# Down projection of a hybrid decoder block: four of 22 chunk pairs in Strassen's form, segment sums kept in DRAM

## The chip, the cores and the metric

The kernel runs on one core of one Trainium2 chip. A core has five engines, each with its own instruction queue: TensorE (PE, matrix multiply, with PEld for its weight loads), VectorE (DVE), ScalarE (ACT), GpSimd (POOL) and SyncE (SP, which here only issues DMAs). Matmuls read SBUF and write PSUM, which has eight banks of 128 x 512 fp32. DVE and ACT read both memories. The metric is the device time of one launch in microseconds (us); before the change it is 1165.92 us, the median of three runs (1165.78 to 1165.96).

## The reference, cut to what matters

One decoder block on x of 256 tokens and 2048 features, in fp32, with one conditioning vector c:

```python
mod = silu(c) @ w_ada + b_ada                     # 2048 x 12288
sh1, sc1, g1, sh2, sc2, g2 = split(mod, 6)
h = rms_norm(x, norm1_g) * (1 + sc1) + sh1
q, k, v, gb, gc, xt = split(h @ w_in, ...)        # 2048 x 6144
attn = causal attention of 8 heads of 128
conv = gb * causal_dwconv(gc * xt, conv_w, conv_b)
x = x + g1 * (concat(norm(attn), norm(conv)) @ w_out)      # 2048 x 2048
h2 = rms_norm(x, norm2_g) * (1 + sc2) + sh2
u_gate, u_up = split(causal_dwconv(h2 @ w_ffn_up, ...), 2) # 2048 x 11264
x = x + g2 * ((silu(u_gate) * u_up) @ w_ffn_down)          # 5632 x 2048
```

The change is in the last product, the down projection: a 256 x 5632 matrix G (the gated activations) times w_ffn_down, 5632 x 2048.

## The kernel before

All of the kernel is one unrolled program. Its matrix work is cut into numbered **slots**, 202 of them before the change. A slot takes one tile of weights (up to four blocks of 128 x 512, 1 MB), loaded from DRAM by SP into one of the `raw` buffers. Every fp32 operand is split into a high and a low part in the format fp32r, and a product is three passes: low part of one operand times high part of the other and the reverse, and high times high. `split_hi` (line 255) makes the high part of a weight tile on ACT, `split_lo` (line 264) the low part on DVE and then asks for the next load (`load_next`). The splits of slot i + 2 are written in the program ahead of the matmuls of slot i (or behind them, for slots in the list `x_first`; the list `hi_late` puts `split_hi` behind the slot's small tasks). `hi` and `lo` have three buffers each, `raw` has six, and a pool of 38 tiles of 128 x 512 fp32 (`t2k`) holds nearly everything else. `CFG` (line 32) is a list of orders and offsets; `at(i, f)` puts a small task into slot i, and its class in `cls` says whether it comes ahead of the splits, and in which order. The main loop (line 1323) writes all of this out slot by slot, so the order on each engine's queue is fixed.

Slots 0 to 47 are the input projection, 48 to 63 the output projection. Then comes the FFN. Its 5632 inner columns are 44 chunks of 128, in 22 **groups** of two chunks. The groups are done in four **segments** (`segs`: 8, 5, 5 and 4 groups). In each segment first comes the up projection of its groups, four slots of about 16 matmuls of 512 columns and 16 of 256 each per group; after it `up_sum`, `up_conv`, `up_silu` and `up_gate` (line 774) finish the group on ACT and DVE and leave its two chunks of G, transposed and split into high and low, in `gT`. Then comes the down projection of the segment: for each column block f of 512 (four of them, taken in the pairs 0 and 1, 2 and 3) slots of up to four chunks, with two row blocks of 128 tokens. A column block has one PSUM bank for each row block, and accumulates over the segment's chunks in `mm_tok` (line 413): for each chunk and row block two passes with the high part of the weights, and after all of them one with the low part. At the end of a segment `evac_down` (line 789) copies a bank into an SBUF tile `dacc` (segment 0, ACT) or adds it (segments 1 and 2, DVE). Ahead of the last segment's sums `gate_down` (line 812) multiplies `dacc` by the gate g2 and adds x; in the last segment `evac_down` multiplies the bank by g2, adds that, and stores. For the last column block g2 is multiplied into the weights instead (`fold`).

The loads of the adaLN weights (`w_ada`, 96 tiles of 1 MB) are spread over the slots by the list `ada`, and DVE or PE accumulates them (`Ada.consume`, line 310). The gate vector g2 is accumulated on DVE in one `raw` buffer during the FFN and spread to all partitions by two small rounds of DMAs on POOL (`sum_rows`, `spread`). PSUM banks come from one pool of eight (`bank`, line 146): four for a group of the up projection, two for each column block of the down projection. A tile that is asked for takes a free buffer of its pool and waits, if need be, for the buffer's last user.

Of the kernel before, what the change touches and what calls it, by code (L numbers as in the profile page):

```python
# [31 lines left out]
CFG = {'ada': [[0, 2, 256, False, 0, 5], [4, 8, 512, False, 64, 8], [5, 0, 2048, False, 109, 18], [3, 8, 512, False, 55, 9],  # L32
# [3 lines left out]
 'bufs': [38, 6, 6, 3, 5],  # L36
# [12 lines left out]
 'segs': [8, 5, 5, 4],  # L49
# [3 lines left out]
 'qk': [[2, 5], [3, 7]],  # L53
# [4 lines left out]
 'slag': [[1, 3], [22, 25]],  # L58
 'hold': [1, 1, 0],
 'evac': [2, 1, 1],  # L60
 'sq': [5, 8, 2],
 'tr': [3, 7, 3],
 'part': 2,
 'up': [[0, 0, 1], [1, 3, 3], [0, 0, 1], [0, 3, 3]],
 'gate': [-16, -17, -6, -9],
# [15 lines left out]
         'evac_down': -1,  # L81
# [23 lines left out]
         'sum_rows': 1},  # L105
 'up0': [[0, 2, 4], [0, 3, 3], [0, 2, 2], [0, 1, 2], [2, 2, 4], [2, 4, 6], [0, 1, 2], [0, 0, 5], [3, 4, 4],
         [0, 2, 3]],
# [15 lines left out]
 'first_hi': True,  # L123
# [1257 lines left out]
```

## Time and profile before

| | us |
|---|---|
| median of 3 runs | 1165.92 |
| the profiled execution, its own time | 1165.9 |
| its span in the trace | 1164.1 |
| PE busy | 1148.0 |
| DVE busy | 920.7 |
| ACT busy | 617.1 |
| POOL busy | 16.9 |
| DMA moved | 320.11 MB, 275 GB/s in the mean |

The span is the time from the first to the last instruction in the trace; some 1.8 us of the device time lie around it. "Busy" is the sum of an engine's instruction times without overlaps. The groups of instructions of the costliest lines are the splits (line 267 on DVE, 445.8 us for 201 of them; line 261 on ACT, 373.9 us) and, on PE, the matmuls of the up projection (lines 861 and 864) and of `mm_tok` (lines 427, 429 and 430).

### The profile page before, as it was taken

The page shows a single profiled execution, that of the slowest core. Times are in us where ns is not written, and L with a number is a line of the kernel's source. Part 1 is how long each engine was busy: PE and PEld are TensorE (multiplying, and loading weights), DVE is VectorE, ACT ScalarE, POOL GpSimd, SP SyncE. Part 2 cuts the span into 40 slices and gives each one's busy share as a digit, 9 for nine tenths or more (in the row PEclk, how much of TensorE's full clock was granted, in tenths as well). Part 3 has the DMA queues.
Part 4 walks back from the last instruction along what each step waited for, and adds up shares of the span by engine and source line. Part 5 has one row for each costly group of instructions (what it writes and reads, how often), then busy time and mean ns, then how long its engine had stood idle before and what let it go on. Part 6 is the DMA issues. An engine that isn't in the chain of part 4 may idle for free.

```text
span 1164.1 us, 15680 instructions
## 1 busy us (share of the span) xinstructions
PE 1148.0 (99%) x6119; PEld 971.6 (83%) x6119; DVE 920.7 (79%) x1030; ACT 617.1 (53%) x889; POOL 16.9 (1%) x34
## 2 busy tenths in 40 slices
PE   6999999999999999999999999999999999999998
PEld 4677778888888889988888888888888888888887
DVE  4789989999999989889876468997556576577767
ACT  5644455667795465566664434545435454335451
POOL 1000000000000000000000000000000000000000
PEclk9999999999999999999999999999999999999999
DMA  9999989999899799975556479995675645675451
GB/s 364 407 416 394 412 328 357 404 351 347 304 357 335 268 333 353 351 252 174 185 191 217 172 273 340 329 344 184 213 233 182 217 163 202 227 235 186 148 178 73
DMA packets 188570, 320.11 MB, mean 275 GB/s; under 512 B 7360, under 2 KB 106132, under 8 KB 183888
## 3 DMA queue, kind: packets, MB, share of 16 engines
q1 hardware_dynamic: 186208, 314.60, 75.7%
q0 software_dynamic: 992, 2.35, 0.6%
q10 hardware_dynamic: 1296, 2.16, 0.5%
q8 instruction: 48, 0.79, 0.3%
q14 instruction: 26, 0.21, 0.0%
HBM read 314.87 MB, written 4.21 MB: 274 GB/s over the span
## 4 chain that ended last, share of the span: by engine, by line
PE 91%; DVE 4%; DMA 3%; ACT 1%; issue 0%; SPq 0%; DVEq 0%; ACTq 0%
PE z L861 25%; PE z L864 13%; PE z L847 4%; DMA raw<-in_w_in_dram 2%; DVE lo L267 2%; PE mk L429 1%; PE mk L430 1%; PE mk L427 1%; PE mx L429 1%; PE mc L429 1%; PE mq L430 1%; PE mg L429 1%; PE mq L429 1%; PE mc L430 1%; PE mx L430 1%; PE mv L429 1%
## 5 line engine op out<-in xcount | busy, mean ns | idle before, releaser
L267 DVE TENSOR_TENSOR lo<-raw,hi 128x2048 fp32r<-128x2048 f32 (+2 forms) x201 | 445.8, 2225 | 142.1 <-ACT hi L261 129.7
L261 ACT ACTIVATE hi<-raw 128x2048 fp32r<-128x2048 f32 (+2 forms) x201 | 373.9, 1865 | 306.7 <-PE z L861 62.9
L861 PE MATMUL z<-h,hi 128*128 128x512 f32 x1280 | 298.5, 390 | 0.0
L861 PEld LDWEIGHTS z<-h,hi 128*128 128x128 f32 x1280 | 237.8, 188 | 47.5
L325 DVE SCALAR_TENSOR_TENSOR ada<-raw,csil,ada 128x512 f32<-128x512 f32 (+3 forms) x167 | 195.9, 1176 | 4.7 <-DMA raw<-in_w_ada_dram 1.2
L864 PEld LDWEIGHTS z<-h,lo 128*128 128x128 f32 x1280 | 159.0, 192 | 4.0 <-issue 0.8
L864 PE MATMUL z<-h,lo 128*128 128x256 f32 x1280 | 160.3, 283 | 0.0
L725 DVE SCALAR_TENSOR_TENSOR uy<-ub,fc,uy 128x254 f32<-128x254 f32 (+1 forms) x176 | 71.4, 480 | 0.2
L757 DVE TENSOR_TENSOR ub<-z,ub 128x256 f32<-128x256 f32 x96 | 34.0, 417 | 36.6 <-ACT ub L754 36.6
L778 ACT ACTIVATE gh<-uy 128x512 fp32r<-128x512 f32 x22 | 13.9, 632 | 66.5 <-DVE uy L776 66.5
L847 PE MATMUL z<-h,hi 128*128 128x256 f32 x256 | 46.6, 285 | 0.4 <-ACT h L679 0.2
L720 ACT ACTIVATE uy<-ub,fc,fc 128x256 f32<-128x256 f32 x88 | 45.6, 601 | 0.0
L754 ACT ACTIVATE ub<-z 128x256 f32<-128x256 f32 x96 | 28.7, 384 | 27.0 <-PE z L861 26.9
L847 PEld LDWEIGHTS z<-h,hi 128*128 128x128 f32 x256 | 40.0, 192 | 0.8 <-ACT h L679 0.5
L847 PE MATMUL z<-h,lo 128*128 128x256 f32 x128 | 36.3, 284 | 0.0
L779 DVE TENSOR_TENSOR gl<-uy,gh 128x512 fp32r<-128x512 f32 x22 | 15.2, 693 | 15.4 <-ACT gh L778 15.4
L429 PE MATMUL mx<-hi,h 128*128 128x512 f32 x64 | 25.8, 403 | 0.4 <-ACT pa_g L439 0.4
L429 PE MATMUL mg<-hi,h 128*128 128x512 f32 x64 | 25.7, 402 | 0.0
L429 PE MATMUL mq<-hi,h 128*128 128x512 f32 x64 | 25.6, 399 | 0.0
L429 PE MATMUL mk<-hi,h 128*128 128x512 f32 x64 | 25.3, 395 | 0.0
L429 PE MATMUL mv<-hi,h 128*128 128x512 f32 x64 | 25.1, 392 | 0.0
L847 PEld LDWEIGHTS z<-h,lo 128*128 128x128 f32 x128 | 24.6, 192 | 0.0
(611 smaller groups left out, 1863.5 us busy)
## 6 DMA issues: line engine op xcount, KB each, us to landing
raw<-in_w_ada_dram SPq DMA_DIRECT2D x96, 1024.0 KB, 7.3
raw<-in_w_ffn_up_dram SPq DMA_DIRECT2D x176, 512.0 KB, 4.8
raw<-in_w_in_dram SPq DMA_DIRECT2D x47, 1024.0 KB, 8.0
raw<-in_w_ffn_down_dram SPq DMA_DIRECT2D x28, 1024.0 KB, 5.0
raw<-in_w_out_dram SPq DMA_DIRECT2D x16, 1024.0 KB, 6.6
raw<-in_w_ffn_down_dram SPq DMA_DIRECT2D x20, 768.0 KB, 4.3
xr<-in_x_dram SPq DMA_DIRECT2D x2, 1024.0 KB, 6.2
x<-in_x_dram SPq DMA_DIRECT2D x8, 256.0 KB, 7.5
```

The lines of the kernel that those rows point to most:

```text
L261: act(hi[:, :nk], t[:, :nk], AF.Copy)
L267: V.tensor_tensor(out=lo[:, :nk], in0=t[:, :nk], in1=hi[:, :nk].bitcast(F32), op=ALU.subtract)
L325: V.scalar_tensor_tensor(out=self.acc, in0=t[:, j, :], scalar=csil[:, i:i + 1], in1=self.acc, op0=ALU.mult, op1=ALU.add)
L429: mm(o, a, hi[:, k, s], start=(first and k == 0), stop=False)
L430: mm(o, b, hi[:, k, s], start=False, stop=False)
L720: act(y[:, s], b[:, s], AF.Identity, bias=bias[:, i + j:i + j + 1], scale=w[2][:, i + j:i + j + 1])
L725: V.scalar_tensor_tensor(out=o[:, d:], in0=v[:, :256 - d], scalar=w[2 - d][:, i + j:i + j + 1], in1=o[:, d:], op0=ALU.mult, op1=ALU.add)
L754: act(c[ft // 2][:, (ft % 2) * 256:(ft % 2) * 256 + 256], zp[grp][ft][:, 256:], AF.Copy)
L757: V.tensor_tensor(out=d, in0=zp[grp][ft][:, :256], in1=d, op=ALU.add)
L847: mm(o, w[:, j, a], h2T[k + j][:, v * 256:v * 256 + 256], start=begins and j == 0 and w is hi and not v, stop=ends and j == 3 and w is lo)
L861: mm(zp[grp][ft], hi[:, j, ft * P:(ft + 1) * P], h2T[k + j], start=begins and j == 0, stop=ends and j == 3)
L864: mm(zp[grp][ft][:, :256], lo[:, j, ft * P:(ft + 1) * P], h2T[k + j][:, :256], start=False, stop=False)
```

## The change

The groups 0, 9, 12 and 14 become **units**. For a unit and one half of the columns (1024 of 2048, `cp`) the product of two row blocks, two chunks and two column blocks is computed as in Strassen's algorithm (in Winograd's variant) with seven block products in place of eight. The sums of blocks of G are made in `up_gate` (tiles `gs`, split again into high and low, seven stationary blocks in `gS`). The sums of weight blocks are made in `split_lo` on DVE, in place in the raw tile: such a tile is used twice, in a slot "A" with three of its blocks as loaded (three products), and in a slot "B" with four sums (four products). A slot B has no load of its own.

The seven products go into seven sums, j of 0 to 6; the ordinary groups ("s") of a segment add their four block products to the sums 0, 1, 3 and 7. So a column half of segments 0 to 2 now uses eight banks. The order of the groups within a segment is written out in `orders`; the two column halves follow each other. Where a sum is complete, `evac_sum` copies its bank to SBUF (ACT for the j in `unit_act`, otherwise DVE), and a DMA on POOL writes it to DRAM, or adds it to what is there (`accum_op`). Near the end of segment 2 and the start of segment 3's up projection `join_load` loads the eight sums of a half on SP, and `join_sum` combines them with eight DVE operations into `dacc`. Weight tiles of segments 0 to 2 now hold two chunks by 1024 columns (`pair_w`) and not up to four chunks by 512. The last segment has five groups (`segs`: 8, 5, 4, 5) and is otherwise computed as before. There are 206 slots. Many numbers of `CFG` are other ones; of its list only those with a part in what follows are shown.

```diff
+CFG = {'orders': [[[4, 's'], [1, 's'], [6, 's'], [0, 'AB'], [3, 's'], [5, 's'], [2, 's'], [7, 's']],
+            [[2, 's'], [1, 'AB'], [3, 's'], [0, 's'], [4, 'AB']], [[0, 's'], [1, 'AB'], [2, 's'], [3, 's']]],
+ 'unit_act': [0, 1, 2, 5, 6, 7],
+ 'join': [[-22, -19], [-17, -14]],
...
-[5, 0, 2048, False, 109, 18]
+[5, 0, 2048, False, 105, 24]
...
- 'segs': [8, 5, 5, 4],
+ 'segs': [8, 5, 4, 5],
...
- 'slag': [[1, 3], [22, 25]],
+ 'slag': [[1, 3], [20, 25]],
...
- 'gate': [-16, -17, -6, -9],
+ 'gate': [-11, -13, -7, -12],
...
+         'evac_sum': -1,
+         'join_load': 1,
+         'join_sum': 2},
...
- 'back': [-28, -26, -15, -19],
+ 'back': [-26, -29, -8, -25],
...
- 'cut': [4, 4],
+ 'cut': [4, 3, 3],
...
@@ -252,21 +259,31 @@
 
     splits, halfway = [], []
 
+    held = []
+
     def split_hi(nk, gate=None):
-        t = take()
+        t = held.pop(0) if nk == "B" else take()
+        n = {"A": 3, "B": 4}.get(nk, nk)
         if gate is not None:
             w = t[:, :nk]
             V.tensor_tensor(out=w, in0=w, in1=gB[gate].unsqueeze(1).to_broadcast([P, nk, 512]), op=ALU.mult)
         hi = sb.tile([P, 4, 512], F32R, tag="hi", bufs=N_HL, name="hi")
-        act(hi[:, :nk], t[:, :nk], AF.Copy)
+        act(hi[:, :n], t[:, :n], AF.Copy)
         halfway.append((t, hi, nk))
 
     def split_lo():
-        t, hi, nk = halfway.pop(0)
+        t, hi, half = halfway.pop(0)
+        nk = {"A": 3, "B": 4}.get(half, half)
         lo = sb.tile([P, 4, 512], F32R, tag="lo", bufs=N_HL, name="lo")
         V.tensor_tensor(out=lo[:, :nk], in0=t[:, :nk], in1=hi[:, :nk].bitcast(F32), op=ALU.subtract)
         splits.append((hi, lo))
-        load_next()
+        if half != "A":
+            load_next()
+            return
+        V.tensor_tensor(out=t[:, 1::2], in0=t[:, 1:3], in1=t[:, 3:4].to_broadcast([P, 2, 512]), op=ALU.add)
+        V.tensor_tensor(out=t[:, 2], in0=t[:, 1], in1=t[:, 2], op=ALU.add)
+        V.tensor_tensor(out=t[:, 0], in0=t[:, 0], in1=t[:, 2], op=ALU.add)
+        held.append(t)
 
 
     csil = const.tile([P, NK], F32, name="csil")
@@ -771,9 +788,27 @@
     def up_silu(grp):
         act(uy[grp][0], uy[grp][0], AF.Silu)
 
+    gS = {}
+
     def up_gate(grp):
         g, u = uy.pop(grp)
         V.tensor_tensor(out=g, in0=g, in1=u, op=ALU.mult)
+        if grp in UNITS:
+
+            s = t2k(f"gs{grp}")
+            gv, sv = (v.rearrange("p (b t) -> p b t", b=4) for v in (g, s))
+            V.tensor_tensor(out=sv[:, :2], in0=gv[:, 1:3], in1=gv[:, 3:4].to_broadcast([P, 2, P]), op=ALU.subtract)
+            V.tensor_tensor(out=sv[:, 2], in0=gv[:, 2], in1=sv[:, 0], op=ALU.add)
+            V.tensor_tensor(out=sv[:, 3], in0=gv[:, 0], in1=sv[:, 2], op=ALU.subtract)
+            parts = []
+            for v, n, w in ((g, 3, "a"), (s, 4, "s")):
+                hi, lo = t2k(f"g{w}h{grp}", F32R), t2k(f"g{w}l{grp}", F32R)
+                act(hi[:, :n * P], v[:, :n * P], AF.Copy)
+                V.tensor_tensor(out=lo[:, :n * P], in0=v[:, :n * P], in1=hi[:, :n * P].bitcast(F32), op=ALU.subtract)
+                parts += [(hi[:, j * P:(j + 1) * P], lo[:, j * P:(j + 1) * P]) for j in range(n)]
+            a12, a22, a11, s1, s3, s2, s4 = parts
+            gS[grp] = (a12, s4, a11), (a22, s3, s2, s1)
+            return
         hi, lo = t2k(f"gh{grp}", F32R), t2k(f"gl{grp}", F32R)
         act(hi, g, AF.Copy)
         V.tensor_tensor(out=lo, in0=g, in1=hi.bitcast(F32), op=ALU.subtract)
@@ -787,39 +822,114 @@
         return seg == len(SEGS) - 1 and f >= CFG["fold"]
 
     def evac_down(seg, f):
-        assert seg < len(SEGS) - 1 or f"gd{f}" in done
-        done.add(f"ed{seg}{f}")
+        assert f"gd{f}" in done
         for t in range(2):
             p = mainp["D", seg, f][t]
-            if seg == 0:
-                dacc[t, f] = t2k(f"da{t}{f}")
-                act(dacc[t, f], p, AF.Copy)
-            elif seg < len(SEGS) - 1:
-                V.tensor_tensor(out=dacc[t, f], in0=p, in1=dacc[t, f], op=ALU.add)
-            else:
-                y = t2k(f"d{f}{t}")
-                w = 256 if f == 3 and t == 1 else 512
-                for h in range(0, 512, w):
-                    s = slice(h, h + w)
-                    p = mainp["D", seg, f][t + h // 256]
-                    if fold(seg, f):
-                        V.tensor_tensor(out=y[:, s], in0=p[:, :w], in1=x1[t, f][:, s], op=ALU.add)
-                    else:
-                        V.tensor_tensor(out=y[:, s], in0=p[:, :w], in1=gB[G2, f][:, s], op=ALU.mult)
-                        V.tensor_tensor(out=y[:, s], in0=y[:, s], in1=x1[t, f][:, s], op=ALU.add)
-                    nc.sync.dma_start(rows_of(t, f)[:, s], y[:, s])
+            y = t2k(f"d{f}{t}")
+            w = 256 if f == 3 and t == 1 else 512
+            for h in range(0, 512, w):
+                s = slice(h, h + w)
+                p = mainp["D", seg, f][t + h // 256]
+                if fold(seg, f):
+                    V.tensor_tensor(out=y[:, s], in0=p[:, :w], in1=x1[t, f][:, s], op=ALU.add)
+                else:
+                    V.tensor_tensor(out=y[:, s], in0=p[:, :w], in1=gB[G2, f][:, s], op=ALU.mult)
+                    V.tensor_tensor(out=y[:, s], in0=y[:, s], in1=x1[t, f][:, s], op=ALU.add)
+                nc.sync.dma_start(rows_of(t, f)[:, s], y[:, s])
 
     def gate_down(f):
-        assert f"ed{len(SEGS) - 2}{f}" in done
         done.add(f"gd{f}")
         for t in range(2):
             V.tensor_tensor(out=dacc[t, f], in0=dacc[t, f], in1=gB[G2, f], op=ALU.mult)
             V.tensor_tensor(out=x1[t, f], in0=dacc[t, f], in1=x1[t, f], op=ALU.add)
 
+    scr = nc.dram_tensor("down_sums", (2, 8, P, 512), F32, kind="Internal").ap()
+    begun, summed = set(), set()
+
+    def evac_sum(seg, cp, j):
+        p, y = mainp["U", seg, cp][j], t2k("pu")
+        if j in CFG["unit_act"]:
+            act(y, p, AF.Copy)
+        else:
+            V.tensor_copy(y, p)
+        if (cp, j) in summed:
+            nc.gpsimd.dma_start(scr[cp, j], y, accum_op=ALU.add)
+        else:
+            nc.gpsimd.dma_start(scr[cp, j], y)
+        summed.add((cp, j))
+
+    joined = {}
+
+    def join_load(cp):
+        joined[cp] = [t2k("ju") if (cp, j) in summed else None for j in range(8)]
+        for j, y in enumerate(joined[cp]):
+            if y is not None:
+                nc.sync.dma_start(y, scr[cp, j])
+
+    def join_sum(cp):
+        p2, q3, p1, q4, q7, q6, q5, x22 = joined.pop(cp)
+        sub, add = ALU.subtract, ALU.add
+        if p1 is not None:
+            for o, x, y, f in ((q6, q6, p1, sub), (p2, p2, p1, add), (q7, q6, q7, sub), (q6, q6, q5, sub),
+                               (q4, q4, q7, sub), (q7, q7, q5, sub), (q3, q3, q6, add), (x22, x22, q7, add)):
+                V.tensor_tensor(out=o, in0=x, in1=y, op=f)
+        for t, n, y in ((0, 0, p2), (0, 1, q3), (1, 0, q4), (1, 1, x22)):
+            dacc[t, 2 * cp + n] = y
+
+    STD = {(0, 0): 0, (0, 1): 1, (1, 0): 3, (1, 1): 7}
+    USE = {"s": (0, 1, 3, 7), "A": (0, 1, 2), "B": (3, 4, 5, 6)}
+
+    def down_std(seg, cp, grp, ends):
+        def go(hi, lo):
+            for low in (False, True):
+                for k in range(2):
+                    for n in range(2):
+                        for t in range(2):
+                            j = STD[t, n]
+                            key = seg, cp, j
+                            a, b = (v[:, t * P:(t + 1) * P] for v in gT[2 * grp + k])
+                            if low:
+                                mm(bank_of(key), a, lo[:, 2 * k + n], start=False, stop=j in ends and k == 1)
+                            else:
+                                mm(bank_of(key), a, hi[:, 2 * k + n], start=key not in begun, stop=False)
+                                begun.add(key)
+                                mm(bank_of(key), b, hi[:, 2 * k + n], start=False, stop=False)
+        return go
+
+    def down_unit(seg, cp, grp, half, ends):
+        def go(hi, lo):
+            st = gS[grp][half == "B"]
+            for low in (False, True):
+                for n, j in enumerate(USE[half]):
+                    key, (a, b) = (seg, cp, j), st[n]
+                    if low:
+                        mm(bank_of(key), a, lo[:, n], start=False, stop=j in ends)
+                    else:
+                        mm(bank_of(key), a, hi[:, n], start=key not in begun, stop=False)
+                        begun.add(key)
+                        mm(bank_of(key), b, hi[:, n], start=False, stop=False)
+        return go
+
+    def bank_of(key):
+        seg, cp, j = key
+        m = mainp.setdefault(("U", seg, cp), {})
+        if j not in m:
+            m[j] = bank(f"u{j}")
+        return m[j]
+
     SEGS, a = [], 0
     for n in CFG["segs"]:
         SEGS.append((a, a + n))
         a += n
+
+    UNITS = {SEGS[i][0] + grp for i, seg in enumerate(CFG["orders"]) for grp, kind in seg if kind != "s"}
+
+    def pair_w(grp, cp):
+        def issue(t):
+            nc.sync.dma_start(t.rearrange("p (k h) f -> p k (h f)", k=2),
+                              w_down[0, 2 * grp * P:(2 * grp + 2) * P, cp * 1024:(cp + 1) * 1024]
+                              .rearrange("(k p) f -> p k f", p=P))
+        return issue
 
     NS, *cut = CFG["split"]
     for seg, (ga, gb_) in enumerate(SEGS):
@@ -876,9 +986,23 @@
             for f in range(4):
                 at(len(slots) + CFG["gate"][f], gate_down, f)
                 at(len(slots) + CFG["back"][f], unspill, f)
+            for cp in range(2):
+                at(len(slots) + CFG["join"][cp][0], join_load, cp)
+                at(len(slots) + CFG["join"][cp][1], join_sum, cp)
         if seg == 1:
             UP_3 = len(slots)
-        cuts = {18: (4, 4, 4, 3, 3), 16: (4, 4, 4, 4), 14: (4, 4, 3, 3), 12: (4, 4, 4), 10: (4, 3, 3), 8: (3, 3, 2), 6: (2, 2, 2)}[kb - ka]
+        if seg < len(SEGS) - 1:
+            for cp in range(2):
+                run = [(ga + g, h) for g, kind in CFG["orders"][seg] for h in (kind if kind != "s" else "s")]
+                last = {j: i for i, (_, h) in enumerate(run) for j in USE[h]}
+                for i, (grp, h) in enumerate(run):
+                    ends = [j for j in USE[h] if last[j] == i]
+                    go = down_std(seg, cp, grp, ends) if h == "s" else down_unit(seg, cp, grp, h, ends)
+                    slots.append((pair_w(grp, cp) if h != "B" else None, 4 if h == "s" else h, go))
+                    for j in ends:
+                        at(len(slots), evac_sum, seg, cp, j)
+            continue
+        cuts = {20: (4, 4, 4, 4, 4), 18: (4, 4, 4, 3, 3), 16: (4, 4, 4, 4), 14: (4, 4, 3, 3), 12: (4, 4, 4), 10: (4, 3, 3), 8: (3, 3, 2), 6: (2, 2, 2)}[kb - ka]
         parts = []
         for f in range(0, 4, 2):
             k = ka
@@ -1200,7 +1324,8 @@
     for e in consume:
         if e[0] == "a" and e[2] == 0 and e[1].n > 1024:
             want(e[1])
-        want(slots[e[1]][0] if e[0] == "w" else e[1].want(e[2]))
+        if e[0] == "a" or slots[e[1]][0] is not None:
+            want(slots[e[1]][0] if e[0] == "w" else e[1].want(e[2]))
 
 
     xr = []
```

More of the change, by code (lines that the diff above doesn't have):

```diff
@@ L28 @@
 SH1, SC1, G1, SH2, SC2, G2 = range(6)
-CFG = {'ada': [[0, 2, 256, False, 0, 5], [4, 8, 512, False, 64, 8], [5, 0, 2048, False, 109, 18], [3, 8, 512, False, 55, 9],
[3 rows of a table removed]
+CFG = {'orders': [[[4, 's'], [1, 's'], [6, 's'], [0, 'AB'], [3, 's'], [5, 's'], [2, 's'], [7, 's']],
+            [[2, 's'], [1, 'AB'], [3, 's'], [0, 's'], [4, 'AB']], [[0, 's'], [1, 'AB'], [2, 's'], [3, 's']]],
+ 'unit_act': [0, 1, 2, 5, 6, 7],
+ 'join': [[-22, -19], [-17, -14]],
+ 'ada': [[0, 2, 256, False, 0, 5], [2, 0, 2048, False, 26, 22], [5, 0, 2048, False, 105, 24],
[3 rows of a table added]
  'bufs': [38, 6, 6, 3, 5],
  'turns': [['c', 0, 2], ['v', 0, 2], ['g', 0, 2], ['x', 0, 2], ['q', 0, 2], ['q', 2, 4], ['c', 2, 4], ['k', 0, 4],
[2 rows of a table removed]
[2 rows of a table added]
            ['q1', 8, 12], ['q1', 12, 16], ['k1', 8, 16], ['v1', 8, 16], ['c0', 8, 16], ['x0', 8, 16], ['g0', 8, 16],
@@ L52 @@
  'conv': [[1, 3, 3, 3, 5, 8, 8, 8], [1, 2, 3, 2, 2, 3, 5, 5]],
- 'qk': [[2, 5], [3, 7]],
+ 'qk': [[3, 5], [3, 7]],
  'norms': [52, 55],
@@ L57 @@
  'vload': 17,
- 'slag': [[1, 3], [22, 25]],
+ 'slag': [[1, 3], [20, 25]],
  'hold': [1, 1, 0],
- 'evac': [2, 1, 1],
+ 'evac': [1, 1, 1],
  'sq': [5, 8, 2],
- 'tr': [3, 7, 3],
+ 'tr': [4, 7, 3],
  'part': 2,
- 'up': [[0, 0, 1], [1, 3, 3], [0, 0, 1], [0, 3, 3]],
- 'gate': [-16, -17, -6, -9],
+ 'up': [[0, 1, 3], [0, 2, 3], [0, 0, 2], [1, 2, 3]],
+ 'gate': [-11, -13, -7, -12],
  'cls': {'add': 2,
@@ L80 @@
          'evac_a': 2,
-         'evac_down': -1,
+         'evac_down': 0,
          'conv_p': 1,
@@ L104 @@
          'ss_cols': -1,
-         'sum_rows': 1},
- 'up0': [[0, 2, 4], [0, 3, 3], [0, 2, 2], [0, 1, 2], [2, 2, 4], [2, 4, 6], [0, 1, 2], [0, 0, 5], [3, 4, 4],
-         [0, 2, 3]],
+         'sum_rows': 1,
+         'evac_sum': -1,
+         'join_load': 1,
+         'join_sum': 2},
+ 'up0': [[1, 2, 4], [0, 3, 4], [0, 2, 2], [0, 1, 3], [2, 2, 4], [2, 4, 6], [1, 2, 2], [0, 1, 5], [3, 3, 4],
+         [0, 2, 4]],
  'la': 2,
@@ L111 @@
  'direct': [4, 0],
- 'spill': [8, 2],
- 'back': [-28, -26, -15, -19],
- 'x_first': [1, 2, 3, 4, 5, 6, 7, 8, 9, 10, 11, 12, 13, 14, 18, 21, 22, 23, 28, 29, 30, 31, 34, 36, 37, 42, 43, 44,
-             45, 47, 48, 49, 50, 51, 53, 56, 60, 61, 66, 68, 73, 74],
+ 'spill': [8, 3],
+ 'back': [-26, -29, -8, -25],
+ 'x_first': [1, 2, 3, 4, 6, 8, 9, 10, 11, 12, 13, 14, 18, 20, 21, 22, 26, 27, 30, 31, 34, 37, 42, 43, 44, 45, 47, 48,
+             49, 50, 51, 53, 56, 60, 61, 62, 65, 66, 67, 69, 74, 80, 82, 86, 87, 90, 103, 108],
  'h_act': True,
  'h_lag': 0,
- 'hi_late': [0, 1, 2, 11, 12, 17, 18, 19, 22, 23, 28, 30, 40, 42, 44, 45, 47, 51, 53, 54, 56, 57, 58, 59, 61, 65, 66,
[4 rows of a table removed]
+ 'hi_late': [1, 2, 3, 9, 11, 12, 17, 18, 19, 20, 22, 23, 28, 30, 31, 39, 42, 44, 45, 47, 49, 51, 53, 54, 56, 57, 59,
[4 rows of a table added]
  'first_hi': True,
- 'cut': [4, 4],
+ 'cut': [4, 3, 3],
  'fold': 3,
```

18 rows, old and new, of the table CFG are left out of this document.

## The prediction, made before the change was run

> **What bounds the kernel now.** I read the page's header and engine lines first, then the chain that ended last, then what TensorE waits for.
>
> ```profile
> span 1164.1 us, 15680 instructions
> ...
> PE 1148.0 (99%) x6119; PEld 971.6 (83%) x6119; DVE 920.7 (79%) x1030; ACT 617.1 (53%) x889; POOL 16.9 (1%) x34
> ...
> PEclk9999999999999999999999999999999999999999
> ...
> PE 91%; DVE 4%; DMA 3%; ACT 1%; issue 0%; SPq 0%; DVEq 0%; ACTq 0%
> ```
>
> TensorE (PE) is busy for 99% of the span, at full clock, and is 91% of the chain. "Busy" could hide gaps, since ends of matmuls are modelled; the table of who waited for whom, PE alone, settles that (columns: us in total, times, longest; first and last of 11 rows, which add up to 11.9 us):
>
> ```profile
> PE pv_ccol L196 <- DMA vcb<-in_c_dram: 4.0, 1, 4.0
> ...
> PE mq L430 <- DVE hl L931: 0.2, 1, 0.2
> ```
>
> No row names a tile of the down projection: wherever the change works, PE waits for nobody, and time there is matmuls times their pitch. The pitch is read from the chain in order of time (start, duration), around segment 2's down projection, and from the busy-time table by stretch (span, then PE, PEld, DVE, ACT, POOL, then clock, DMA share, GB/s):
>
> ```profile
> 969.51 3.65 PE z L861 x16
> ...
> 1027.57 3.63 PE z L861 x16
> ...
> 0.00:100.00 100.00, 88.59 (x478) 64.09 (x478) 72.10 (x99) 55.58 (x77) 7.33 (x20) 1.00 1.02 396
> ...
> 850.00:900.00 50.00, 50.00 (x274) 42.74 (x274) 27.41 (x28) 22.17 (x21) 2.46 (x5) 1.00 0.64 210
> ...
> 973.00:1027.00 54.00, 54.00 (x240) 44.76 (x239) 32.79 (x35) 23.94 (x22) 0.00 (x0) 1.00 0.71 235
> ```
>
> Up projection ends at 969.51 + 3.65 = 973.16 and begins again at 1027.57. Between them lie segment 2's 240 matmuls (10 chunks x 4 column blocks x 2 row blocks x 3 passes): 54.41 / 240 = **0.2267 us each**, back to back. A slot of 24 is 5.44 us. DVE is busy 61% and ACT 44% of that stretch.
>
> **Removed from PE.** A pair of chunks and a half of the columns is 2 x 2 x 2 block products of 3 passes: 24 matmuls. `down_unit` has 7 products, three in slot A (9 matmuls, 2.04 us) and four in slot B (12, 2.72 us): 21. The four pairs in this form, with two halves each, save 4 x 2 x 3 = 24 matmuls: 24 x 0.2267 = **-5.44 us**. All other pairs keep their count. The sums on the stationary side and on the weights run on DVE, so nothing is added to PE.
>
> The last segment grows from 4 groups to 5, and its last column block runs one row block in 256-wide halves:
>
> ```profile
> 1158.42 0.48 PE m('D', 3, 3)1_9703 L427 x4
> ```
>
> A half is 0.12 us. Twelve more of them in place of six full matmuls cost 12 x 0.12 - 6 x 0.2267 = +0.08 us. The tail behind the last matmul is the same code.
>
> The Trainium skill, in TensorE: Matmul & The Clock Gate, section "Wait — 56ns, not 53.3ns?", gives 215.7 ns from start to start for 512 columns at full clock. By that the saving would be an estimated 24 x 0.2157 = 5.18 us; the trace's 226.7 ns decides.
>
> **Added on DVE and ACT.** Durations from the timelines of the two engines:
>
> ```profile
> 644.63 1.92 ACT L261 ACTIVATE hi<-raw 128x2048 fp32r<-128x2048 f32 x1 [3.52 <-PE m('D', 0, 0)1_5609 L430]
> 646.46 0.57 ACT L796 ACTIVATE da<-m('D', 0, 0)0_5608 128x512 f32<-128x512 f32 x1
> 646.93 0.59 ACT L796 ACTIVATE da<-m('D', 0, 0)1_5609 128x512 f32<-128x512 f32 x1
> 650.07 1.92 ACT L261 ACTIVATE hi<-raw 128x2048 fp32r<-128x2048 f32 x1 [2.56 <-issue]
> 651.89 0.57 ACT L796 ACTIVATE da<-m('D', 0, 1)0_5640 128x512 f32<-128x512 f32 x1
> ...
> 986.80 1.49 ACT L261 ACTIVATE hi<-raw 128x1536 fp32r<-128x1536 f32 x1 [1.78 <-PE m('D', 2, 0)1_8406 L430]
> ...
> 646.58 2.29 DVE L267 TENSOR_TENSOR lo<-raw,hi 128x2048 fp32r<-128x2048 f32 x1 [2.92 <-ACT hi L261]
> ...
> 681.38 2.35 DVE L325 SCALAR_TENSOR_TENSOR ada<-raw,csil,ada 128x2048 f32<-128x2048 f32 x1
> ...
> 980.62 1.76 DVE L267 TENSOR_TENSOR lo<-raw,hi 128x1536 fp32r<-128x1536 f32 x1 [0.56 <-ACT hi L261]
> ...
> 996.10 0.69 DVE L798 TENSOR_TENSOR da<-m('D', 2, 0)0_8405,da 128x512 f32<-128x512 f32 x1 [0.92 <-PE m('D', 2, 0)0_8405 L427]
> ```
>
> DVE: eight A tiles each add a `lo` of three blocks (1.76) and three sums of weights (1024, 512 and 512 wide; the first lies between 0.69 and 1.76, I take 1.22; together 2.60): 8 x 4.36 = 34.9 us. `up_gate` of four groups adds small sums and a wider split, about 1.5 us each: 6. `join_sum`: 16 x 0.69 = 11.0. Twelve of the 48 bank copies of `evac_sum` (j of 3 and 4) are DVE's: 8.3. Sixteen adds of the old `evac_down` go: -11.0. Net +49 us. ACT: `hi` of three blocks 8 x 1.49 = 11.9, 36 bank copies instead of 8: 28 x 0.58 = 16.2, the gates some 2 to 3: about +31 us. In the down stretch above DVE has 21 us idle of 54 and ACT 30, so the sums fit; what counts is order.
>
> *Unit chain.* `hi` and `lo` have three buffers, so the split of a slot can begin when the slot three earlier ends. B's `hi` also waits for A's `hi`, `lo` and the sums, all in the one raw tile. The tightest place is the second half of segment 0, slots 105 to 110, where DVE also accumulates the gate vector (2.35 us in slots 105, 106, 108, 109). With slot 105 at 0: A's `hi` 5.44 to 6.93, `lo` to 8.7, sums to 11.3, B's `hi` to 13.2; its matmuls start at 18.36: **5.2 us to spare**. Behind it slot 110's `hi` can start at 16.32 and ends at 18.24, needed at 21.08; its `lo` ends near 20.5, needed only for the last eight matmuls, at 24.7. Nothing here is late, so I cost the chain at 0; uncovered it would be at most the 2.60 us of sums per unit, 8 x 2.60 = 21 us.
>
> *PSUM banks.* All eight are used by one column half. Where a unit is not last in the order (segments 0 and 2), four banks were emptied slots ago when the next half begins. Segment 1 ends with a unit: bank 7 is free, banks 0, 1, 2 close with A, the rest with B. Slot B, its start at 0: ACT first makes the `hi` of three blocks (1.49), then copies 0, 1, 2, ending near 2.1, 2.6 and 3.1 (starts 0.47 apart, as at 646.46 and 646.93). The next half writes one bank every 0.45 us from 2.72: the second at 3.17, the third at 3.62, the fourth at 4.08. **About 1 us to spare**. That holds if the oldest free bank is taken; the rows speak for it: slot end 650.07, copy of that slot's bank at 651.89, and no PE wait, so the next slot did not take the newest. Value taken 0; with newest-first reuse six turnovers of 1 to 3 us each, 6 to 18 us.
>
> *Less held back.* No `dacc` tile lives through segments 1 and 2 (eight tiles of the 2 KB pool fewer); the sums' copies and the join's 16 tiles take their place.
>
> **Added on the queues.**
>
> ```profile
> raw<-in_w_ffn_down_dram SPq DMA_DIRECT2D x28, 1024.0 KB, 5.0
> ...
> x<-out_dram SPq DMA_DIRECT2D x8, 256.0 KB, 5.2
> out_dram<-d SPq DMA_DIRECT2D x7, 256.0 KB, 2.3
> ...
> gate_sums<-adar POOLq DMA_DIRECT2D x8, 2.0 KB, 3.4
> ...
> 879.46 1.91 POOL L348 DMA_DIRECT2D gate_sums<-adar  x4 [222.49 <-ACT adar L346]
> 883.00 0.55 POOL L354 DMA_DIRECT2D ada<-gate_sums  x1 [1.64 <-DMA gate_sums<-adar]
> ```
>
> POOL issues 48 transfers at about 0.5 us each, 24 us on an engine that is 1% busy. Behind them on POOL wait the gate vector's row sums and spread (slots 147 and 152), needed first some 30 slots later. On SP the 16 loads of `join_load` stand before weight loads; the second eight, in slot 175, wait for sums that leave in slot 174: copy, issue, landing of 3.4 to 5.2 us, some 10 us after slot 174 begins. SP stops for perhaps 5 us. Weight tiles have six buffers, one held by the gate vector, so five loads are ahead: 27 us. Hidden.
>
> No row shows an accumulating DMA. The first stretch shows the engines full (share 1.02) at 396 GB/s, so a plain 256 KB takes 0.66 us of all engines; with the old sum read back, I take twice that, 1.3 us. Ends: 0.66, and 5.2 (the slow landing of a whole 256 KB). At 1.3 us segment 1's down stage (51.7 us of PE) has 10 weight loads at 2.65 and 16 sums at 1.3: 47 us. Full, but fitting, with five loads of cover behind it.
>
> **The sum.** -5.44 + 0.08 + 0 = -5.36 on the profiled execution's own 1165.9 us (span 1164.1 and 1.8 around it), which is also the median 1165.92: **1160.5 us**.
>
> **Rivals.**
> 1. *Partly given back.* The moved splits, the changed order lists and the denser ACT queue cost 0.1 to 0.6 us per unit where a `hi` or a bank comes late; 8 units: 1 to 5 us, 1161.5 to 1165.4, middle 1163. For it: the 1 us margin at segment 1's banks, and that I worked only the tightest places. Against it: 5.2 us in the chain.
> 2. *Slower: accumulating DMAs starve the weight loads.* Place: segments 1 and 2, down stage. With D us of all engines per sum, segment 1 needs 26.5 + 16 D in 51.7 us with 27 us of cover: PE begins to wait at D = 3.3, and the change loses from 3.6. At D = 5 the wait is 80 + 26.5 - 78.7 = 28 us: 1188. Against it: 5.2 us was latency, not occupation.
> 3. *Descriptors late.* POOL builds these transfers; were it held back, SP would stand at the join and stop weight loads. Four sums must land before slot 175's loads; at 10 us each SP stands some 35 us against 27 us of cover: +8, or 1168.5. Against it: POOL's issues at 879.46 took 0.48 us each while DVE was 55% busy. The Trainium skill, SBUF — State Buffer, section "Who interferes with whom", says that DVE copies in a two-port mode lock GpSimd out, and that `tensor_tensor` does not have this mode; the `lo` row, 2.29 us for 2048 elements, bears that out with about one element a cycle, and the new DVE work is of this kind.
> 4. *Better than the count.* The other edited lists (order of ada loads, turns, offsets) act on the 11.9 us of waits, nearly all at the start; 1 to 2.5 us could go: 1158 to 1159.3.
> 5. *It does not do what it says.* The count of matmuls follows from the code, so this would be the PE count not falling by some 24: 1166. I give it 0.01.
>
> **How the numbers follow.** Forecast (1159.3 to 1161.5) 0.62; rival 1 0.21; rivals 2 and 3 together 0.08; rival 4 0.08; rival 5 0.01. A measurement of this kernel can tell about 0.2%, 2.3 us, from no change. Faster than 1163.6: 0.62 + 0.08 + 0.11 of rival 1 = 0.81. Within: 0.10 + 0.01 = 0.11. Slower than 1168.2: 0.08. Range 1158.6 to 1164.6: it leaves out rivals 2, 3 and 5 (0.09), the top of 1 (0.03) and the bottom of 4 (0.03).
>
> **What would show it.** PE's matmul records about 24 lower; still no PE wait in the down stretches; in segment 1 bank copies of 0, 1, 2 ending before the next half's matmuls; join loads landing before slot 177. I would be wrong with PE rows waiting for `hi`, for `pu` copies, or ACT's `hi` waiting for raw tiles right after the accumulating DMAs.

## The result, and the profile after

The changed kernel takes **1159.84 us** in the median of six runs (1159.48 to 1160.88), the kernel before 1165.99 (1165.78 to 1166.25): 6.15 us less, a ratio of 0.9948 with a 95% interval of 0.9935 to 0.9961. On another chip, beside the experiments below, the two were 1160.52 and 1166.33. The prediction was 1160.5, in a range of 1158.6 to 1164.6. The profiled execution took 1160.0 us, with a span of 1158.2.

The page of the changed kernel, in the lines that answer to those shown of before:

```profile
span 1158.2 us, 15897 instructions
...
PE 1144.3 (99%) x6101; PEld 968.6 (84%) x6101; DVE 968.0 (84%) x1087; ACT 641.6 (55%) x925; POOL 53.6 (5%) x82
...
q0 software_dynamic: 6880, 14.94, 5.7%
...
PE 92%; DVE 3%; DMA 2%; ACT 1%; issue 1%; SPq 0%; DVEq 0%; ACTq 0%
...
down_sums<-pu POOLq DMA_DIRECT2D x48, 256.0 KB, 7.3
...
ju<-down_sums SPq DMA_DIRECT2D x16, 256.0 KB, 6.9
```

PE still bounds the kernel and has 18 records less: 24 block-product matmuls gone, and 12 half-width ones in place of 6 full ones come with the longer last segment. DVE grew by 47 us and ACT by 24, and still PE hardly waits (who waited for whom, PE alone; the first and the last of 8 rows):

```profile
PE pv_ccol L203 <- DMA vcb<-in_c_dram: 3.8, 1, 3.8
...
PE z L957 <- ACT h L696: 0.2, 1, 0.2
```

The eight rows add up to 9.9 us, against 11.9 before, and as before none is in a down projection. Such a table understates PE's losses, because the ends of matmuls are modelled: a loss of 0.38 us in the last up projection, seen below, stands in no row of it. To see where the time went I take the first matmul of each stage from PE's timeline, for both kernels. "From counts" is the number of matmuls times 0.2267 us. The last stage is taken to the end of the last matmul.

| stage (us) | before | after | from counts |
|---|---|---|---|
| all ahead of the first up projection | 426.84 | 425.88 | |
| down, segment 0 | 87.04 | 85.68 | 378: 85.69 |
| down, segment 1 | 54.40 | 53.07 | 228: 51.69, and 1.4 for the gate's row sums, which lay in the next stage before, where they took 1.2 |
| up and down, segments 2 and 3, to the last matmul's end | 299.65 | 297.60 | |
| of this, the up projection with 20 slots, after | | 111.51 | 111.13, as in segment 1 |

Up projections of segments 0 and 1 take 181.27 and 111.13 us in both kernels. The balance: -5.44 (24 matmuls) + 0.11 (half-width matmuls) - 0.96 (ahead of the FFN) + 0.38 (last up projection) = -5.91 us; the span shrank by 5.9. Two small terms are left out of it that cancel: the row sums cost 0.2 us more, and the stretch behind the last matmul is 0.2 us shorter. So the saving came in full. Of the other terms, -0.96 and +0.38 partly cancel in this execution, and both were put to the test.

### The profile page after: what moved, and what is told of

Read it like the earlier page. It is cut to its first block, busy times and chain, and to the rows that moved or that the text cites. A ratio compares the mean times of both kernels' runs of the same rounds, so it can differ in the third digit from the quotient of the medians.

```text
span 1158.2 us, 15897 instructions
## 1 busy us (share of the span) xinstructions
PE 1144.3 (99%) x6101; PEld 968.6 (84%) x6101; DVE 968.0 (84%) x1087; ACT 641.6 (55%) x925; POOL 53.6 (5%) x82
## 3 DMA queue, kind: packets, MB, share of 16 engines
q0 software_dynamic: 6880, 14.94, 5.7%
## 4 chain that ended last, share of the span: by engine, by line
PE 92%; DVE 3%; DMA 2%; ACT 1%; issue 1%; SPq 0%; DVEq 0%; ACTq 0%
PE z L971 23%; PE z L974 12%; PE u L896 4%; PE u L892 4%; PE u L894 4%; PE z L957 4%; PE mk L446 1%; PE mk L447 1%; PE mk L444 1%; PE ada L336 1%; DVE lo L278 1%; PE mx L446 1%; PE mq L447 1%; PE mg L446 1%; PE u L908 1%; PE u L906 1%
## 5 line engine op out<-in xcount | busy, mean ns | idle before, releaser
L278 DVE TENSOR_TENSOR lo<-raw,hi 128x2048 fp32r<-128x2048 f32 (+1 forms) x205 | 458.2, 2246 | 102.5 <-ACT hi L271 95.2
L271 ACT ACTIVATE hi<-raw 128x2048 fp32r<-128x2048 f32 (+1 forms) x205 | 383.7, 1884 | 273.8 <-DMA raw<-in_w_in_dram 70.2
L974 PEld LDWEIGHTS z<-h,lo 128*128 128x128 f32 x1280 | 159.0, 192 | 3.4 <-DVE lo L278 0.3
L896 PE MATMUL u<-hi,gl 128*128 128x512 f32 x208 | 80.9, 389 | 0.0
L894 PE MATMUL u<-hi,gh 128*128 128x512 f32 x208 | 80.9, 389 | 0.0
L892 PE MATMUL u<-lo,gh 128*128 128x512 f32 x208 | 51.4, 389 | 0.0
L896 PEld LDWEIGHTS u<-hi,gl 128*128 128x128 f32 x208 | 39.0, 188 | 8.1
L894 PEld LDWEIGHTS u<-hi,gh 128*128 128x128 f32 x208 | 39.0, 188 | 8.1
L892 PEld LDWEIGHTS u<-lo,gh 128*128 128x128 f32 x208 | 39.0, 188 | 8.1
L856 POOL DMA_DIRECT2D down_sums<-pu x32 | 27.8, 1169 | 270.7 <-ACT pu L852 254.4
```

Of the source, the lines that this page charges most:

```text
L271: act(hi[:, :n], t[:, :n], AF.Copy)
L278: V.tensor_tensor(out=lo[:, :nk], in0=t[:, :nk], in1=hi[:, :nk].bitcast(F32), op=ALU.subtract)
L892: mm(bank_of(key), a, lo[:, 2 * k + n], start=False, stop=j in ends and k == 1)
L894: mm(bank_of(key), a, hi[:, 2 * k + n], start=key not in begun, stop=False)
L896: mm(bank_of(key), b, hi[:, 2 * k + n], start=False, stop=False)
L974: mm(zp[grp][ft][:, :256], lo[:, j, ft * P:(ft + 1) * P], h2T[k + j][:, :256], start=False, stop=False)
```

## The experiments

All were timed beside the kernel before on their own chip, and "against before" below is the difference of the two medians there.

**Is it the matmuls?** One run takes only the units away:

```diff
-CFG = {'orders': [[[4, 's'], [1, 's'], [6, 's'], [0, 'AB'], ...
+CFG = {'orders': [[[4, 's'], [1, 's'], [6, 's'], [0, 's'], ...
```

(and the same for the other three; slot numbers in the lists moved along). Without units a column half has four sums and not eight, so this run also has 24 transfers of sums in place of 48, and `join_sum` has nothing to add.

> All 17 groups of segments 0 to 2 in the ordinary form, everything else of the changed kernel kept (order lists moved to the same slots, sums in DRAM, join, wide weight tiles). Theory (the gain is 24 matmuls at 0.2267 us, all sums hidden): 5.4 us slower than the changed kernel, near 1165.3; PE's waits as in the changed kernel. Rival (the gain comes from the wide weight tiles, the freed buffers and the moved lists): within 1 us of the changed kernel, near 1160 to 1161.

1164.67 us, -1.70 against before (ratio 0.9985, 0.9976 to 0.9994). Taking the units out costs 4.1 to 4.5 us, by the changed kernel's -5.81 and -6.15 on its two chips: less than the 5.4 expected. In its trace the down projections of segments 0 to 2 take 87.04, 54.40 and 43.52 us, which are 384, 240 and 192 matmuls back to back, and the last up projection 111.13: all 5.44 us are back, and the loss at the join (0.38 us in one profile of the changed kernel, 1.13 in another) is gone. The rival falls: wide weight tiles, freed buffers and sums in DRAM can together be worth 1.70 us at most, and the next test shows that even these come from elsewhere.

**The lists for the first 64 slots.** Forward (they alone put back as they were) and mirrored (they alone put into the kernel before):

```diff
- 'qk': [[3, 5], [3, 7]],
+ 'qk': [[2, 5], [3, 7]],
- 'evac': [1, 1, 1],
+ 'evac': [2, 1, 1],
- 'tr': [4, 7, 3],
+ 'tr': [3, 7, 3],
...
```

> The changed kernel with the lists that act before slot 64 as they were before (turns, qk, evac, tr, x_first and hi_late below 64, order of the ada entries, span of one of them). The trace has the first down projection starting 0.98 us earlier after the change, 607.30 against 608.28. Theory (these lists make that difference): 0.7 to 1.2 us slower than the changed kernel, first down projection again near 608.3. Rival (the difference is scatter of the first loads from run to run): no difference beyond 0.4 us in the median.

1161.65 us, -4.72 against before and so 1.1 to 1.4 us slower than the changed kernel, with the first up projection at 427.5 us and the first down projection at 608.7.

> The kernel before, with the changed kernel's lists for the slots below 64 (turns, qk, evac, tr, x_first and hi_late below 64, order of the ada entries, span of one of them) and nothing else of the change. Theory (these lists are worth about 1.2 us, by the eight profiles with them, 425.4 to 426.5, against the two without, 426.84 and 427.47): first up projection begins at 425.4 to 426.5, 0.7 to 1.5 us faster than the kernel before. Rival (scatter): begins near 427, no faster than 0.3 us.

1164.60 us, -1.78 against before (ratio 0.9983, 0.9975 to 0.9992). Where the first up projection begins, by the rows of its first line (kernel before, changed, lists put back, kernel before with the new lists; the first number behind the colon and comma is the start):

```profile
L847 PE MATMUL z<-h,hi x256: 282/284/387, 426.8 to 473.6; 128*128 128x256 f32 x128
```
```profile
L957 PE MATMUL z<-h,hi x256: 278/283/387, 425.9 to 472.6; 128*128 128x256 f32 x128
```
```profile
L957 PE MATMUL z<-h,hi x256: 279/283/384, 427.5 to 474.2; 128*128 128x256 f32 x128
```
```profile
L847 PE MATMUL z<-h,hi x256: 281/283/386, 425.7 to 472.4; 128*128 128x256 f32 x128
```

Over all profiles of this study, eleven with the new lists lie between 425.4 and 426.5, the two with the old ones at 426.8 and 427.5. So these lists are worth about 1.2 us in the traces and 1.1 to 1.8 in the medians, and have nothing to do with Strassen's form. Which waits they shorten is shown only in part: the wait of `x1t` for ACT's `ada`, 0.4 us, is in both profiles with the old lists and in none with the new ones. The run without units and this one agree (-1.70 and -1.78): the rest of the change, as far as the run without units has it, is neutral.

**Are the accumulating DMAs hidden?** Here the sums overwrite, so the output leaves out parts of segments 0 and 1:

```diff
-            nc.gpsimd.dma_start(scr[cp, j], y, accum_op=ALU.add)
+            nc.gpsimd.dma_start(scr[cp, j], y)
```

> The sums of segments 1 and 2 overwrite those of the segment before in DRAM instead of being added to them, so the output lacks segments 0 and 1 of the down projection in part; all else is the same. Theory (the accumulating DMAs are hidden): same time within 0.5 us; packets of these 32 transfers near 0.65 us of all 16 engines each, like the plain ones, instead of 1.52; the stall of some 0.3 us at the join may go. Rival (the accumulating DMAs still cost PE time through late weight loads): faster by 1 us or more.

1159.87 us, -6.50 against before, 0.4 to 0.7 us faster than the changed kernel on its two chips. The intervals don't tell that apart, but the stage times do: the last up projection is back at 111.13 us. Queue 0's share of the span falls to 3.3%:

```profile
q0 software_dynamic: 4832, 14.94, 3.3%
```

From 5.7% that is 2.4% of 1158 us = 28 us for 32 transfers: adding costs 0.87 us of all 16 engines on top of a plain 256 KB. The plain price is (3.3% - 0.6% of the kernel before) x 1158 / 48 = 0.65; an accumulating one so costs 1.52. (The sum over the packets in the traces gives the same 1.52, and 1.47 in the second profile of the changed kernel.) What it delays is seen in DVE's timeline at the first `join_sum`, in the changed kernel and in this one (start, duration; in brackets the idle time ahead and what ended it):

```profile
996.83 2.29 DVE L278 TENSOR_TENSOR lo<-raw,hi 128x2048 fp32r<-128x2048 f32 x1 [0.96 <-ACT hi L271]
1005.20 5.15 DVE L875 TENSOR_TENSOR ju<-ju 128x512 f32<-128x512 f32 x8 [6.08 <-DMA ju<-down_sums]
```
```profile
994.49 2.29 DVE L278 TENSOR_TENSOR lo<-raw,hi 128x2048 fp32r<-128x2048 f32 x1 [3.16 <-ACT hi L271]
997.39 5.16 DVE L875 TENSOR_TENSOR ju<-ju 128x512 f32<-128x512 f32 x8 [0.61 <-DMA ju<-down_sums]
```

With accumulation DVE stands idle 6.08 us in front of the sum; without it, 0.61. SP issues the eight loads that the sum needs from 989.60 to 997.32 us with accumulation, from 982.46 to 991.69 without. Two weight loads just ahead of them on SP's queue took 4.2 and 5.5 us to issue with accumulation, 0.9 and 0.4 without; what held them isn't shown. The splits queued on DVE behind the sum come late, and PE pays a little for it at 1049 us.

**Can the join be placed better?** In `join` each pair is the load and the sum of one column half. I first read it as loads and sums of both halves, so the first edit moved something else than its expectation says: the *loads* of the second half, from slot 177 to 179.

```diff
- 'join': [[-22, -19], [-17, -14]],
+ 'join': [[-22, -19], [-15, -14]],
```

> The first join_sum two slots later (slot 179 in place of 177), nothing else. Theory (DVE stood 6.1 us at the join for loads that were late behind the accumulating DMAs, and the splits queued behind it then came late: 0.38 us of PE): the last up projection takes 111.13 us again in place of 111.51, 0.3 to 0.4 us faster than the changed kernel. Rival (the loads themselves hold up the weight tiles on SP): no difference, 111.5.

1164.18 us, -2.15 against before, so 3.7 us slower than the changed kernel beside it (1160.52). The idle time at the first sum stays (7.11 us), DVE now waits at the second `join_sum` too, and PE loses 4.1 us in that stage (115.27 us), so neither side of the expectation was tested:

```profile
1030.56 5.16 DVE L875 TENSOR_TENSOR ju<-ju 128x512 f32<-128x512 f32 x8 [3.97 <-DMA ju<-down_sums]
```

Then the edit that was meant, by two slots and by one:

```diff
- 'join': [[-22, -19], [-17, -14]],
+ 'join': [[-22, -17], [-17, -14]],    # e7
+ 'join': [[-22, -18], [-17, -14]],    # e9
```

> Each pair in 'join' is the load and the sum of one half; here the first half's join_sum stands two slots later, in slot 177 in place of 175, loads and the second half as they are. Theory (DVE stands 6 to 8 us in front of the first join_sum because its loads land late, and the splits queued behind it come late; this is what costs PE 0.4 to 1.1 us in the last up projection): that stage takes 111.13 to 111.3 us in place of 111.51 and 112.26, the kernel is 0.4 to 1 us faster than the changed one. Rival (DVE has simply too much work there, wherever the sum stands): 111.5 or more.

> The same with the first half's join_sum one slot later (176 in place of 175). Theory: about half of the idle time ahead of it goes, the last up projection takes 111.13 to 111.6 us. Rival (too much work): 111.5 or more, as in the run beside it.

Two slots: 1164.30 us, -2.08 against before, last up projection 115.46 us. One slot: **1159.86 us, -6.52 against before** (ratio 0.9943, 0.9930 to 0.9955), 111.35 us. The theory fails for the first: DVE no longer stands in front of the sum for its loads, but it stands all the same, for the next `hi`, and does the sum after that, when the next splits are due:

```profile
1001.49 2.29 DVE L278 TENSOR_TENSOR lo<-raw,hi 128x2048 fp32r<-128x2048 f32 x1 [3.17 <-ACT hi L271]
1012.11 2.29 DVE L278 TENSOR_TENSOR lo<-raw,hi 128x2048 fp32r<-128x2048 f32 x1 [8.33 <-ACT hi L271]
1014.32 5.15 DVE L875 TENSOR_TENSOR ju<-ju 128x512 f32<-128x512 f32 x8
```

The rival (too much work, wherever the sum stands) fails with the second, whose sum begins in the same gap with 1.57 us of idle time ahead of it:

```profile
1001.29 2.29 DVE L278 TENSOR_TENSOR lo<-raw,hi 128x2048 fp32r<-128x2048 f32 x1 [2.77 <-ACT hi L271]
1005.15 5.15 DVE L875 TENSOR_TENSOR ju<-ju 128x512 f32<-128x512 f32 x8 [1.57 <-DMA ju<-down_sums]
```

With the loads landing as late as they do here, there is one gap in DVE's queue that takes the 5.15 us, between about 1004 and 1012 us. In the changed kernel the sum stands ahead of a split and holds it back while it waits for its loads; one slot later that split goes first; two slots later the gap has passed. (With plain writes, above, the sum ran from 997.39 to 1002.55 and cost PE nothing either.) One slot later than the changed kernel fits best, but its gain over that kernel (0.4 to 0.7 us between differences taken on different chips) is smaller than the intervals tell apart.

Not all of the two slots' loss is waiting. After PE's longest wait there (2.1 us, up to 1040.5), the granted clock of its profile is at one half from 1042.0 to 1045.4 us, and matmuls of 512 columns start 0.427 us apart; by their number that is an estimated 1.5 of the 4.3 us (span, PE, PEld, DVE, ACT, POOL, clock, DMA share, GB/s):

```profile
1042.00:1045.40 3.40, 3.40 (x12) 2.92 (x12) 3.37 (x8) 3.40 (x6) 0.00 (x0) 0.50 0.84 288
```

**How much spare has a unit?** Each A tile's `lo` is computed three times, 3.5 us more of DVE per tile:

```diff
+        for _ in range(2):
+            V.tensor_tensor(out=lo[:, :nk], in0=t[:, :nk], in1=hi[:, :nk].bitcast(F32), op=ALU.subtract)
```

> Each slot A's lo is computed three times, the same values: 2 x 1.76 = 3.5 us more of DVE for each of the eight tiles, 28 us in all, between the split of A and the sums. Theory (5.2 us to spare in the chain of a unit where DVE is busiest): the three down projections of segments 0 to 2 stay at 85.68, 53.07 and 42.16 us within 0.3 us each. Rival (DVE already at its limit there, as the 1.27 us that the third unit of segment 0 cost suggest): 1 us or more lost in segment 0, 3 us or more in all.

1183.26 us, 22.7 more than the changed kernel beside it. By stage:

| down projection | added on DVE | lost on PE |
|---|---|---|
| segment 0 (2 tiles) | 7.0 | 1.59 |
| segment 1 (4 tiles) | 14.1 | 14.97 |
| segment 2 (2 tiles) | 7.0 | 6.73 |

The theory falls. The rival's figures are met (1 us or more in segment 0, 3 or more in all), but not its reason: of segment 0's loss, 1.4 us fall on the first half's unit, between 625 and 629 us, and none on the second half's, beside the gate vector. Segment 0 swallows most of the added work, segments 1 and 2 next to nothing. In segment 1 the granted clock is at one half from 830.6 to 837.3 us and from 868.1 to 871.4; by the spacing of the matmuls there an estimated 3 to 4 of the 14.97 us are this, and the rest is waiting. The waits name the sums of G and the copies of the banks, not the weights' split alone (PE's waits; two of 18 rows):

```profile
PE u L910 <- ACT gah L808: 3.8, 1, 3.8
PE u L910 <- ACT pu L854: 3.0, 1, 3.0
```

In the changed kernel the same place is just in time. DVE in segment 1 runs from 807.3 to 824.6 us with one pause of 0.23 us; its end, ahead of the second unit (DVE, then PE's first matmul of slot A and the first that reads `gsl`):

```profile
812.67 6.15 DVE L278 TENSOR_TENSOR lo<-raw,hi 128x2048 fp32r<-128x2048 f32 x3
818.86 1.22 DVE L283 TENSOR_TENSOR raw<-raw 128x1024 f32<-128x1024 f32 x1
820.12 0.69 DVE L284 TENSOR_TENSOR raw<-raw 128x512 f32<-128x512 f32 x1
820.85 0.69 DVE L285 TENSOR_TENSOR raw<-raw 128x512 f32<-128x512 f32 x1
821.45 0.68 DVE L795 TENSOR_TENSOR uy<-uy,uy 128x512 f32<-128x512 f32 x1
...
823.95 0.69 DVE L807 TENSOR_TENSOR gsl<-gs,gsh 128x512 fp32r<-128x512 f32 x1 [0.23 <-ACT gsh L806]
```
```profile
825.04 0.39 PE L908 MATMUL u<-hi,gah 128*128 128x512 f32 x1
...
825.72 0.39 PE L910 MATMUL u<-hi,gsl 128*128 128x512 f32 x1
```

Three splits, the weight sums, the gate product of the segment's last group and its sums follow each other; the last stationary blocks are ready at 824.64. That is 0.4 us before slot A begins, at 825.04, and 1.1 us before the first matmul that reads them, at 825.72.

**More units.** Two more, and two in segment 0 at a distance (slot numbers in the lists moved along):

```diff
# e4_six_units: segment 0 and segment 2
-[0, 'AB'], [3, 's'], [5, 's'], [2, 's'], [7, 's']
+[0, 'AB'], [3, 's'], [5, 'AB'], [2, 's'], [7, 's']
-[[0, 's'], [1, 'AB'], [2, 's'], [3, 's']]
+[[0, 's'], [1, 'AB'], [2, 's'], [3, 'AB']]
# u5_seg0: segment 0
-[[4, 's'], [1, 's'], [6, 's'], [0, 'AB'], [3, 's'], [5, 's'], [2, 's'], [7, 's']]
+[[4, 's'], [1, 'AB'], [6, 's'], [0, 's'], [3, 's'], [5, 'AB'], [2, 's'], [7, 's']]
```

> Two more units, group 5 of segment 0 and group 3 of segment 2 (the last in its order). Theory (each unit is worth 6 matmuls, 1.36 us, while DVE and ACT keep up): 2.7 us faster than the changed kernel, near 1157.1. Rival (DVE is at its limit around the gate vector in segment 0 and at the join): less than half of it, 1158.5 or more, with PE waiting for hi or lo there.

> Segment 0 with two units, groups 1 and 5, four slots apart, in place of group 0 alone: five units. Theory (a unit costs PE nothing where the splits of the one before have caught up): segment 0's down projection 84.3 us, 1.36 us faster than the changed kernel. Rival (the second unit of segment 0 doesn't pay beside the gate vector's accumulation, whatever the distance): 85.4 or more, as with the units two slots apart.

Six units: 1169.11 us, 2.74 slower than before, with twelve matmuls fewer than the changed kernel: far from the theory's 1157.1. Segment 0's down projection takes 85.61 us where 372 matmuls are 84.33, segment 2's 46.05 where 180 are 40.81, and the last up projection 116.35 instead of 111.13. In segment 2 the second unit is the group that finishes last, and PE waits for its sums:

```profile
PE u L908 <- ACT gah L806: 1.3, 1, 1.3
...
PE z L974 <- DVE lo L278: 2.8, 2, 2.3
```

Five units: 1161.42 us, 0.9 slower than the changed kernel beside it. Segment 0 takes 85.73 us, 1.4 over its count (1.3 with six units), and the up projection behind it 112.61 in place of 111.13. So in both runs a second unit of segment 0 gives nearly all of its 1.36 us back. This doesn't settle the theory of distance, nor its rival: the edit also moved the first unit two slots earlier, to the second place behind the up projection, and most of the loss is there. By the starts of the matmuls, 1.3 of the 1.4 us are lost between 611 and 623 us, in that unit's slots and the next, ahead of the gate vector's accumulation; the unit four slots on loses nothing in the first half and 0.1 in the second.

> The changed kernel as it is, on the same chip as the next three, so that they can be compared with it directly. Both theories: 6.1 us faster than the kernel before; the input and output projections (all ahead of the first up projection) end at 425.4 to 426.5, as in the other profiles with the new lists.

1160.52 us, -5.81 against before, and the first up projection at 425.96. The same program lost 1.1 us in its last up projection in this profile (112.26), where the first one lost 0.38: the wait at the join differs between these two profiles. The changed kernel's six runs spread over 1.4 us, the six of before beside them over 0.5; on the other chips the kernel before spread over 1.0 to 1.9 us, so a wider spread isn't shown.

## Why the prediction was right, and where it was wrong

**The saving** (24 matmuls at 0.2267, -5.44) is right to a hundredth: -1.36, -2.72 and -1.36 in the three segments, and the run without units has them back. The 226.7 ns of the trace, and not the 215.7 ns cited beside it, is the one that adds up. Half-width matmuls: +0.11 for a predicted +0.08.

**The work on DVE and ACT** was sized well (DVE +47.3 us for +49, ACT +24.5 for +31) and costed at 0, which is right for the down projections. But the step "the tightest place is the second half of segment 0 ... 5.2 us to spare" is wrong as a statement on the whole. That place was roomy: B's `hi` is done there at 663.89 us, 4.5 us before its first matmul at 668.35, and 3.5 us more of DVE cost it nothing. The unit of the first half had 2.8 us (622.72 to 625.51), and the tight place, segment 1, I didn't work. I counted the chain of a unit's weights, and left out that the segment's last group still has its convolution, gate product and sums of G on the same DVE queue. These had 1.1 us to spare.

**PSUM banks**: no wait, as forecast, but with less room than "about 1 us". Not one `hi` but two stood ahead of the copies on ACT:

```profile
826.10 3.29 ACT L271 ACTIVATE hi<-raw 128x2048 fp32r<-128x2048 f32 x2
829.28 1.08 ACT L852 ACTIVATE pu<-u 128x512 f32<-128x512 f32 x2
```

The first copy, some 0.58 us of that pair, is done near 829.86; the next half began at 829.80 and came to its second bank at 830.25. That is 0.4 us. By their own rows in the trace the second and third copy end at 830.36 and 830.85, and their banks are written from 830.71 and 831.16: 0.35 and 0.3 us.

**The queues.** The price of an accumulating DMA, 1.3 us by estimate, is 1.52; rival 2 (from 3.3 us on) had no chance to come. Rival 3's "the new DVE work is of this kind" leaves out twelve bank copies, which are copies and not `tensor_tensor`; they took 0.69 us each, like a `tensor_tensor` of that size. The step that failed here is "Hidden" for the join. I looked at SP's queue and its loads (with the wrong slots: they stand in 172 and 177, not in 175), and forgot DVE's: `join_sum` waits for the loads in the middle of a queue of splits. DVE stood 6.08 us there in the profiled execution and 7.80 in another, and PE lost 0.38 and 1.1 us. A cost of 0 was taken where 0.4 to 1.1 us was measured.

**Rival 4** was no alternative to the forecast but an addition to it: the lists for the first slots gave 1.1 to 1.8 us. So the median lies 0.7 us under the forecast because this term was left out of the sum, and not more because the join took part of it back. That the forecast came this near is so in part luck: two terms that it put at nothing have opposite signs. The sum as it should have stood: -5.44 + 0.1 - 1.2 + 0.4 to 1.1, or -5.4 to -6.1.

**Rivals 1 and 3** didn't show in the changed kernel's down projections. What rival 1 describes (a `hi` or a bank that comes late) is what the fifth and sixth units ran into.

## What to carry to other kernels

Fewer matmuls pay at their full pitch only as long as the engine that prepares their operands is ahead; here 3 matmuls saved per unit and column half (0.68 us) cost DVE 4.4 us, and a fifth and a sixth unit gave nothing where they were put. Work the spare of *every* stage that a change touches, and with all that shares the queue there: the stage with the most listed work was not the tight one. An instruction that waits for a DMA on a queue in order holds everything behind it, so place it where the data is certainly there and the queue has a gap; here one slot was worth at most 0.7 us, and two slots cost 4.

## What the runs showed of the hardware

An accumulating 256 KB DMA into DRAM took 1.52 us of all 16 engines, a plain one 0.65. Its packets are half the size (2048 bytes where plain ones have 4096): queue 0 has 6880 packets with 32 accumulating transfers and 4832 with plain ones, 64 more for each of them, at the same 14.94 MB. POOL also took longer to issue one (changed kernel, then the run with plain writes; least, median and greatest ns):

```profile
L856 POOL DMA_DIRECT2D down_sums<-pu x32: 835/1150/1868, 826.5 to 995.9; - x32
```
```profile
L856 POOL DMA_DIRECT2D down_sums<-pu x32: 539/542/568, 827.1 to 991.4; - x32
```

The spread up to 1868 ns is there with accumulation alone; whether DVE's work or the DMA rings cause it wasn't tried. The granted clock was 0.994 to 1.0 in the mean of every run, but it is not a constant within one. Two profiles show it at one half for 3.4 us or 6.8 us in the middle of the kernel, with matmuls of 512 columns 0.427 us apart in place of 0.227: the run with the first sum two slots later (1042.0 to 1045.4 us, behind a wait of PE of 2.1 us), and the run with three splits (830.6 to 837.3 and 868.1 to 871.4 us, at waits of 3.8 and 2.6 us). Other waits of that length were followed by no such stretch (2.2 and 3.0 us in segment 2 of the run with three splits, 2.3 us with six units), so what brings it on isn't shown.
